# A transformer block with 32 experts on one core: output projection by feature, two gates summed on TensorE, a ninth weight place

## The chip, the cores and the metric

The kernel runs on one core of a Trainium2 chip. The metric is the device time of one execution in microseconds (us); the figure quoted is the median of three runs. TensorE is called PE below, VectorE DVE, ScalarE ACT, GpSimd POOL and SyncE SP. DVE, ACT and POOL work element by element, PE multiplies matrices, and SP issues almost all of the DMA transfers.

## The reference

One block of a model on 256 tokens of 1024 features, float32, depth 1. In outline:

```
mod = silu(c) @ w_ada + b_ada                      # 6 vectors of 1024
sh1, sc1, ga1, sh2, sc2, ga2 = split(mod)
h = rmsnorm(x, g_norm1) * (1 + sc1) + sh1
q_lat, kv_lat, k_pe, sb_qkv, gate_a, gate_b = split(h @ w_in)
o_mla = latent attention(q_lat, kv_lat, k_pe)      # 8 heads, softmax, chunk-causal
o_sb  = stick-breaking attention(sb_qkv)           # 8 heads
merged = sigmoid(gate_a) * (o_mla @ w_o_mla) + sigmoid(gate_b) * (o_sb @ w_o_sb)
x = x + ga1 * (merged @ w_out)
h2 = rmsnorm(x, g_norm2) * (1 + sc2) + sh2
x = x + ga2 * moe(h2)                              # top 4 of 32 experts
```

Each expert is a clamped SwiGLU with `w_gate_up` of 1024 x 2048 and `w_down` of 1024 x 1024, so the experts' weights are 32 x 12 MB and nearly all of what is read from memory.

## The kernel before, in words

**Weights.** Everything is streamed from memory once. First come 27 units of up to 2 MB (`load_units`, issued by SP at L174) with the modulation, projection and attention weights, through a ring of five, later six places. Then come 192 units of 2 MB for the experts (`expert_weights`, L804): per pair of experts eight units of `w_gate_up` and four of `w_down`. They go through eight places: the six of the ring and two more (`places`, L790 and L791). A unit is issued when the unit that held its place has been read for the last time.

**Order of the work.** The program is one long function. A scheduler decides the order of instructions on each engine from a simulated timeline, except where an engine is named in `ordered`; there the order of the program is kept. `ordered` holds DVE, ACT and PE in the front, DVE and PE around the last output projection, and PE in the first pair of experts. All operations of PE, DVE and ACT go through one helper and so have one line, L79; the trace tells them apart by the names of their tiles.

**Front (L178 to L452).** `x` arrives with the tokens on the partitions. 16 PE transposes (`p_xt`) turn it, and the factor of the norm is put in when the transposed tiles are copied to `xT`. The two vectors of the first norm's modulation are summed on PE (`first_sums`: eight matmuls into four 32-row strips of `p_mod`; `first_modulation`: two matmuls by ones). Float32 products are made of three matmuls in a faster type, on a high and a low half (`split`, `mm3`). `h @ w_in` for the latent and the stick-breaking columns runs in eight steps over j (`p_in`). The 32 rotary key columns are not among them; they come later as eight plain float32 matmuls (`p_kpe`, L505).

**Attention and merge (L475 to L786).** The other four modulation vectors (`ada2`: 1 and 2 for the second norm, 0 and 3 for the gates ga1 and ga2) are summed on DVE: 32 products of 128x1024 with a row sum (`modulation_sum`, L701), 16 of them for the gates, hung behind splits of weights in the gate and merge steps. The merge runs over eight feature blocks m: `merge_of` makes gate_b (`p_gb`) and both output products (`p_m`) and from them `m_hi` and `m_lo`; `project` (L759) adds the block to the output projection with the tokens on the partitions:

```
for t in range(2):
    for d in range(2):
        mm3(accs[t][d], (rows_of(m_hi, m, t), rows_of(m_lo, m, t)), w[d], m == 0, False)
```

**Router (L807 to L914).** `ga1` has been spread over all partitions (`rows_of_column`: diagonal matrices on ACT, a matmul by ones `p_row`, a copy on ACT). DVE multiplies the projection by it and adds `x`, which is loaded again (L784). 16 PE transposes (`p_ht`) make `x2T`, from which `p_lg` makes the router's logits, separately for the two halves of the tokens. `residual` puts `x` itself into the accumulators with four matmuls by the identity.

**Experts (L917 to L1142).** The tokens of four experts at a time are gathered by matmuls with one-hot matrices (`gather`, `p_xg`); each expert makes `p_gate` and `p_up` (`gate_up`), a hidden tile (`swiglu`, `hidden`) and `p_y` (`down`). `scaled` multiplies by ga2 and `combine` adds the pair's results to the tokens. In the first two pairs there are also: the broadcast of ga2 (`rows_of_column`, L1130), and the biases of the down projections (`down_biases`, L1081: one DMA of `b_down` on ACT's queue, four matmuls `acc<-rest,gwT`).

Of the kernel before, what the change touches and what calls it, by code (L numbers as in the profile page):

```python
# [36 lines left out]
UNIT = 4096  # L37

# [25 lines left out]
def block_kernel(ctx: ExitStack, tc: tile.TileContext, a, out):  # L64
# [96 lines left out]
    def load_units(n):  # L161
        ins = None
        for _ in range(n):
# [14 lines left out]
    xT = m8([128, 8, T], "xT")  # L178
    x = x8([128, 2, D], "x")
    for t in range(2):  # L180
        SP.dma_start(out=x[:, t], in_=a["x"][:, t])
# [76 lines left out]
    ss = ep.tile([128, 2], F32, name="ss")  # L258
    r1 = ep.tile([128, 2], F32, name="r1")
    scaled = s4([128, 4, 128], "scaled")  # L260
    scaled_ident, rb = scaled[:, 0:2], scaled[:, 2:4]

    def transpose(q):
        ps = [pb("p_xt") for _ in range(2)]
        for t in range(2):
            for i in range(4):
                tr(ps[t][:, i * 128:(i + 1) * 128], x[:, t, (4 * q + i) * 128:(4 * q + i + 1) * 128], ident)
        return ps

# [59 lines left out]
    h_hi, h_lo = h8(0, [128, 8, T], "h_hi"), h8(1, [128, 8, T], "h_lo")  # L329
# [9 lines left out]
    def first_modulation(j, p, acc):  # L339
# [549 lines left out]
    with tc.issue_after(counted.ins):  # L889
        for t in range(2):  # L890
            halves(t, slice(0, 256))
# [352 lines left out]
```

## Time and profile before

| | |
|---|---|
| three runs | 1193.01, 1194.36, 1196.43 us; median 1194.36 us |
| the profiled execution | 1196.56 us, of which the span of the trace is 1194.9 us |
| busy share of the span | PE 91%, DVE 33%, ACT 17%, POOL 4% |
| TensorE clock granted, mean | 0.987 of full speed |
| bytes moved | 460.96 MB, mean 386 GB/s |

The times of the rows further on are microseconds from the start of the span. A share is of the stretch named; a wait is put down to what released it last. Matmuls are pipelined: the distance from one start to the next, not the duration of one, is what it costs in a row of equal ones.

### The profile page before, as it was taken

To read this page: it belongs to the slowest core of one execution; us is meant where nothing else is said; L and a number is where in the kernel's file an instruction comes from. 1 tells how busy PE (TensorE), PEld (TensorE's weight loads), DVE (VectorE), ACT (ScalarE), POOL (GpSimd) and SP (SyncE) were. 2 spreads that over 40 slices of the span, in tenths; PEclk is the share of its full clock that TensorE was granted. 3 is DMA by queue.
4 is the path that set the end of the run, shared out by engine and by line. 5 is a ranking of instruction groups with operands and counts; after the bars stand their busy time and mean duration, and the time that the engine had idled before them with its cause. 6 is when DMAs were issued, how large, how long until landed. Compare 5 with 4: busy or idle time off the path is not lost.

```text
span 1194.9 us, 15656 instructions
## 1 busy us (share of the span) xinstructions
PE 1086.7 (91%) x6549; PEld 611.5 (51%) x6550; DVE 390.2 (33%) x863; ACT 204.7 (17%) x453; POOL 42.6 (4%) x154
## 2 busy tenths in 40 slices
PE   9989998988999999998898889888988998899877
PEld 8968777953536344453534253425352635263524
DVE  5578787762212212221222121212121212121212
ACT  3486664641000000100000000000000000000000
POOL 6000000010000000000000000000000000000000
PEclk9999998999989999999999999999999999999999
DMA  9954459889989999999999999999999999999995
GB/s 384 364 197 182 176 209 419 296 278 409 395 368 430 426 426 428 426 428 428 426 428 427 428 426 427 427 428 428 428 426 426 425 429 428 427 427 427 428 427 215
DMA packets 34267, 460.96 MB, mean 386 GB/s; under 512 B 4080, under 2 KB 4336, under 8 KB 6032
## 3 DMA queue, kind: packets, MB, share of 16 engines
q1 hardware_dynamic: 33408, 458.65, 92.1%
q10 hardware_dynamic: 784, 1.25, 0.4%
q8 instruction: 53, 0.87, 0.3%
q14 instruction: 22, 0.18, 0.0%
HBM read 458.84 MB, written 1.05 MB: 385 GB/s over the span
## 4 chain that ended last, share of the span: by engine, by line
PE 47%; DMA 47%; DVE 3%; ACT 1%; issue 1%; ACTq 0%; DVEq 0%
DMA we<-in_w_gate_up_dram 27%; DMA we<-in_w_down_dram 18%; PE p_gate L79 10%; PE p_y L79 9%; PE p_up L79 9%; PE acc L79 4%; PE p_in L79 3%; PE p_g L79 2%; PE p_gb L79 2%; PE p_xg L79 1%; PE p_m L79 1%; DMA unit<-in_stream_dram 1%; PE p_r L79 1%; PE p_z L79 1%; PE p_sc L79 1%; PE p_mod L79 1%
## 5 line engine op out<-in xcount | busy, mean ns | idle before, releaser
L79 PE MATMUL p_gate<-we,xg 128*64 128x512 f32 x1024 | 277.2, 607 | 43.1 <-DMA we<-in_w_gate_up_dram 42.5
L79 PE MATMUL p_up<-we,xg 128*64 128x512 f32 x1024 | 270.0, 593 | 0.0
L79 PE MATMUL p_y<-we,hid 128*64 128x256 f32 x2048 | 234.2, 382 | 30.7 <-DMA we<-in_w_down_dram 27.0
L79 PEld LDWEIGHTS p_y<-we,hid 128*64 128x64 f32 x2048 | 156.4, 137 | 101.1 <-DVE late L79 27.8
L79 PEld LDWEIGHTS p_gate<-we,xg 128*64 128x64 f32 x1024 | 69.5, 137 | 183.5 <-issue 103.9
L79 PEld LDWEIGHTS p_up<-we,xg 128*64 128x64 f32 x1024 | 76.8, 137 | 143.3 <-issue 143.0
L79 DVE TENSOR_SCALAR g<-p_gate 128x512 f32<-128x512 f32 x32 | 22.1, 691 | 365.2 <-PE p_gate L79 365.2
L79 DVE TENSOR_TENSOR late<-p_y,ga 64x256 f32<-64x256 f32 x128 | 54.0, 422 | 210.1 <-PE p_y L79 208.7
L79 ACT ACTIVATE s<-g 128x512 f32<-128x512 f32 x32 | 20.1, 630 | 444.3 <-DVE g L79 444.3
L79 DVE TENSOR_TENSOR lo<-unit,hi 128x512 fp32r<-128x512 f32 x114 | 74.2, 657 | 40.0 <-ACT hi L79 35.0
L79 ACT ACTIVATE hi<-unit 128x512 fp32r<-128x512 f32 x114 | 68.3, 604 | 43.6 <-PE p_gb L79 9.4
L79 PE MATMUL acc<-late,rest 128*128 128x256 f32 x256 | 62.4, 386 | 5.3 <-DVE late L79 5.3
L79 PEld LDWEIGHTS acc<-late,rest 128*128 128x128 f32 x256 | 46.1, 190 | 21.3 <-DVE late L79 9.8
L79 ACT ACTIVATE rest<-p_pw 128x512 f32<-128x512 f32 x16 | 9.6, 597 | 260.6 <-PE acc L79 148.7
L79 ACT ACTIVATE xg<-p_xg,cols 128x256 f32<-128x256 f32 x32 | 16.8, 565 | 153.8 <-PE p_xg L79 153.8
L79 DVE TENSOR_SCALAR xg<-p_xg,cols 128x256 f32<-128x256 f32 x32 | 16.7, 539 | 74.0 <-PE p_pw L79 37.3
L79 DVE SCALAR_TENSOR_TENSOR unit<-unit,cb 128x1024 f32<-128x1024 f32 x32 | 38.7, 1217 | 0.0
L79 PE MATMUL p_xg<-oh,x2h 128*128 128x256 f32 x128 | 36.1, 314 | 2.6 <-ACT xg L79 2.5
L79 PEld LDWEIGHTS p_xg<-oh,x2h 128*128 128x128 f32 x128 | 24.1, 188 | 17.5 <-issue 12.7
L79 DVE COPY hid<-p_h 128x512 f32<-128x512 f32 x32 | 22.1, 692 | 32.0 <-PE p_h L79 31.5
L79 PE MATMUL p_xg<-oh,x2l 128*128 128x256 f32 x128 | 31.9, 281 | 0.0
L79 PE MATMUL p_in<-h_hi,hi 128*128 128x256 f32 x104 | 30.6, 294 | 0.0
(332 smaller groups left out, 1138.9 us busy)
## 6 DMA issues: line engine op xcount, KB each, us to landing
we<-in_w_gate_up_dram SPq DMA_DIRECT2D x128, 2048.0 KB, 35.2
we<-in_w_down_dram SPq DMA_DIRECT2D x62, 2048.0 KB, 32.1
unit<-in_stream_dram SPq DMA_DIRECT2D x15, 2048.0 KB, 8.6
unit<-in_stream_dram SPq DMA_DIRECT2D x6, 1872.0 KB, 13.7
unit<-in_stream_dram SPq DMA_DIRECT2D x3, 1024.0 KB, 11.3
we<-in_w_down_dram SPq DMA_DIRECT2D x2, 1024.0 KB, 34.1
we<-in_w_down_dram SPq DMA_DIRECT2D x4, 512.0 KB, 25.3
unit<-in_stream_dram SPq DMA_DIRECT2D x1, 1920.0 KB, 7.9
```

The costliest lines, as they stand in the source:

```text
L79: ins = f(*args, **kw)
```

## The change

`x` is handed over with the features on the partitions and loaded straight into `xT`, both times. The first norm's sum of squares is made with matmuls by ones, and its factor for all 256 tokens is computed on 128x256 tiles. The rotary key columns join the steps of `in1`. The sums of `ada2` for the two gates go to PE (`modulation`), after m = 2 and m = 4; the DVE sums stay for the second norm's two vectors, all in the first gate's steps. The diagonals of `rows_of_column` go from ACT to POOL and the copies behind them to DVE; `ga1` is not spread any more. `project` has the features on the partitions, so that the gate ga1 is one number per partition; the sum with `xT` is `x2T` at once, and 16 matmuls by the identity turn it into the accumulators. `b_down` lies in the space of `y` now, and `pw` and `ohw` beside it. `x2h` and `xg` change places in memory, and the room of `h_hi` and `h_lo` becomes a ninth place for expert weights.

```diff
-    x = x8([128, 2, D], "x")
+    xT = x8([128, 8, T], "xT")
...
+    def first_norm():
         for t in range(2):
...
+            for k in range(4):
+                mm(acc1[3][:, 0:T], lhsT=ones, rhs=sq[:, k], start=(t + k == 0), stop=(t + k == 4))
+        v, r, u = (norms[:, i] for i in range(3))
+        V.tensor_scalar(v, acc1[3][:, 0:T], 1.0 / D, EPS, op0=OP.mult, op1=OP.add)
+        S.activation(r, v, AF.Ln)
+        S.activation(r, r, AF.Exp, scale=-0.5)
+        V.scalar_tensor_tensor(u, r, -0.5, v, op0=OP.mult, op1=OP.mult)
+        V.tensor_mul(u, u, r)
+        V.scalar_tensor_tensor(r, u, 1.5, r, op0=OP.add, op1=OP.mult)
...
             for i in range(4):
-                S.activation(diag[:, i], ident, AF.Copy, scale=col[:, 4 * d + i:4 * d + i + 1])
+                G.tensor_scalar(diag[:, i], ident, col[:, 4 * d + i:4 * d + i + 1], None, op0=OP.mult)
             p = bank("p_row")
             mm(p, lhsT=ones, rhs=diag.rearrange("p i n -> p (i n)"), start=True, stop=True)
-            S.activation(o[:, d * 512:(d + 1) * 512], p, AF.Copy)
+            V.tensor_copy(o[:, d * 512:(d + 1) * 512], p)
...
-            if j == 0 and n == 0:
-                xt1 = transpose(1)
+            if n == 3:
+                mm3(acc1[6][0:32, T:2 * T], (w[0][:, 128:160], w[1][:, 128:160]), (h_hi[:, j], h_lo[:, j]), False, j == 7)
...
+    def modulation(n):
+        accs_ = gp.tile([128, 2, 512], F32, tag="cb", name="accr", bufs=1)
+        for d in range(2):
+            w = where["ada2", (n, d)].rearrange("p (k n) -> p k n", k=8)
+            weighted_sums([w[:, k] for k in range(8)], accs_[:, d], pc("p_ada"))
+            p = pc("p_sum")
+            for i in range(4):
+                mm(p[:, i:i + 1], lhsT=accs_[:, d, i * 128:(i + 1) * 128], rhs=ones[:, 0:1], start=True, stop=True)
+            c = slice(4 * d, 4 * d + 4)
+            V.tensor_add(cols2[:, n, c], p[:, 0:4], b2[:, n, c])
...
-        for t in range(2):
-            for d in range(2):
-                mm3(accs[t][d], (rows_of(m_hi, m, t), rows_of(m_lo, m, t)), w[d], m == 0, False)
+            w.append(split(where["out", m][:, c]))
+        for f in range(8):
+            c = slice((f % 4) * 128, (f % 4 + 1) * 128)
+            mm3(acc2[f // 2][:, (f % 2) * T:(f % 2 + 1) * T], (w[f // 4][0][:, c], w[f // 4][1][:, c]),
+                (m_hi[:, m], m_lo[:, m]), m == 0 and f % 2 == 0, m == 7)
...
+        if m in (2, 4):
+            modulation(0 if m == 2 else 3)
...
-    places[5:5] = [(ring_c, 7), (ring_c, 8)]
+    places[5:5] = [(ring_c, 7), (ring_c, 8), (keep, 9)]
...
+    for f in range(8):
+        V.scalar_tensor_tensor(x2T[:, f], acc2[f // 2][:, (f % 2) * T:(f % 2 + 1) * T], cols2[:, 0, f:f + 1], xT[:, f],
+                               op0=OP.mult, op1=OP.add)
+        if f % 4 == 3:
+            accs[f // 4] = [pa(f"acc{t}{f // 4}") for t in range(2)]
+
+            for t in range(2):
+                for i in range(f - 3, f + 1):
+                    mm(accs[f // 4][t][:, (i % 4) * 128:(i % 4 + 1) * 128], lhsT=x2T[:, i, t * 128:(t + 1) * 128],
+                       rhs=ident, start=(i % 4 == 0), stop=False, skip_group_check=True)
+
+    for f in range(8):
+        g = slice(32 * (f % 4), 32 * (f % 4) + 32)
+        mm(p_lg[g, 0:T], lhsT=wr[:, f], rhs=x2T[:, f], start=(f < 4), stop=(f >= 4), skip_group_check=True)
...
-    bd = rest[0:E, 1024:2048]
+    bd = late[0:E, 0:D]
```

The change moves instructions on several engines. Three places are shown: the gates' sums, the down biases, and the loads of expert weights.

On DVE of the kernel before, in the merge, near 190 us: the gates' sums (`unit,cols<-unit,cb`) stand four in a row between splits (`lo`) and the merge's own products (`gb`, `ma`).

```order
L79 TENSOR_TENSOR lo<-unit,hi 128x512 x5
L79 SCALAR_TENSOR_TENSOR unit,cols_1240<-unit,cb 128x1024 x4
L79 TENSOR_TENSOR gb<-p_m,gb 128x256
L79 TENSOR_TENSOR ma<-p_m,gat_1238 128x256
L79 TENSOR_TENSOR lo<-unit,hi 128x512 x2
L79 SCALAR_TENSOR_TENSOR unit,cols_1240<-unit,cb 128x1024
L79 TENSOR_TENSOR lo<-unit,hi 128x512
L79 SCALAR_TENSOR_TENSOR unit,cols_1240<-unit,cb 128x1024
L79 TENSOR_TENSOR cols_1240<-cols_1240,small 128x4
L79 TENSOR_TENSOR ma<-ma,gb 128x256
```

On PE after the change, where `modulation` of the first gate has its second half: the eight matmuls of `p_ada` stand between those of `project(2)` (`acc`). DVE has no `unit,cb` row left in the merge.

```order
L80 MATMUL acc<-m_lo,hi 128x256
L80 MATMUL acc<-m_hi,lo 128x256
L80 MATMUL acc<-m_hi,hi 128x256
L80 MATMUL p_ada<-unit,scb 32x512 x8
L80 MATMUL acc<-m_lo,hi 128x256
```

So the sums leave DVE's queue and come into PE's, four groups of eight, each with four matmuls `p_sum` further on.

On PE of the kernel before, between the third expert (bias rows `bgu`) and the fourth (`p_gate`, `p_up`): the down biases.

```order
L79 MATMUL p_gate<-bgu,sel 128x512
L79 MATMUL p_up<-bgu,sel 128x512
L79 MATMUL p_pw<-ident,rest 128x128 x4
L79 MATMUL acc_1966<-rest,gwT 128x512
L79 MATMUL acc_1967<-rest,gwT 128x512
L79 MATMUL acc_1968<-rest,gwT 128x512
L79 MATMUL acc_1969<-rest,gwT 128x512
L79 MATMUL p_gate<-we,xg 64x512 x7
L79 MATMUL p_up<-we,xg 64x512 x6
```

And after the change:

```order
L80 MATMUL p_gate<-we,xg 64x512 x13
L80 MATMUL p_up<-we,xg 64x512 x12
L80 MATMUL p_gate<-we,xg 64x512
L80 MATMUL p_up<-we,xg 64x512 x2
L80 MATMUL p_gate<-we,xg 64x512 x2
L80 MATMUL p_up<-we,xg 64x512 x2
L80 MATMUL p_gate<-bgu,sel 128x512
L80 MATMUL p_up<-bgu,sel 128x512
L80 MATMUL acc_2953<-late,gwT 128x512
L80 MATMUL acc_2967<-late,gwT 128x512
L80 MATMUL acc_2954<-late,gwT 128x512
L80 MATMUL acc_2968<-late,gwT 128x512
```

The four matmuls with `gwT` are now behind the whole of the fourth expert's `p_gate` and `p_up`.

On SP of the kernel before, the first loads of expert weights, eight ahead of the first that waits for an expert (the row of four `w_down`):

```order
L784 DMA x<-in_x_dram 128x2048
L174 DMA unit<-in_stream_dram 128x4096
L804 DMA we<-in_w_gate_up_dram 128x4096
L174 DMA unit<-in_stream_dram 128x4096
L804 DMA we<-in_w_gate_up_dram 128x4096 x7
L804 DMA we<-in_w_down_dram 128x4096 x4
L804 DMA we<-in_w_gate_up_dram 128x4096 x4
```

After the change:

```order
L770 DMA xT<-in_x_dram 128x2048
L172 DMA unit<-in_stream_dram 128x4096
L790 DMA we<-in_w_gate_up_dram 128x4096
L172 DMA unit<-in_stream_dram 128x4096
L790 DMA we<-in_w_gate_up_dram 128x4096 x5
L790 DMA we<-in_w_down_dram 128x4096
L790 DMA we<-in_w_gate_up_dram 128x4096 x2
L790 DMA we<-in_w_down_dram 128x4096 x3
L790 DMA we<-in_w_gate_up_dram 128x4096 x5
```

Nine loads stand ahead of the last three of `w_down` now, with one `w_down` before the last two of `w_gate_up`.

## Rows read from the trace of the kernel before

**Rows 1.** Windows: PE, PEld, DVE, ACT, POOL busy (instructions), PEclk, DMA share, GB/s
```profile
260.00:270.00 10.00, 9.03 (x44) 3.52 (x40) 1.28 (x4) 0.84 (x2) 3.75 (x4) 1.00 0.57 211
340.00:350.00 10.00, 10.00 (x29) 2.95 (x29) 2.08 (x3) 0.00 (x0) 0.00 (x0) 0.66 0.74 318
360.00:390.00 30.00, 29.31 (x208) 18.33 (x210) 7.89 (x17) 2.40 (x5) 0.00 (x0) 1.00 1.00 428
400.00:1160.00 760.00, 686.10 (x3982) 329.32 (x3980) 161.16 (x323) 37.27 (x65) 13.78 (x51) 1.00 1.01 427
```

**Rows 2.** Timeline of SP's queue: start, us from first to last issue, loads
```profile
208.98 35.49 SPq L804 DMA_DIRECT2D we<-in_w_gate_up_dram  x7
263.41 15.05 SPq L804 DMA_DIRECT2D we<-in_w_down_dram  x4
...
349.84 29.56 SPq L804 DMA_DIRECT2D we<-in_w_gate_up_dram  x8
387.33 4.56 SPq L804 DMA_DIRECT2D we<-in_w_down_dram  x2
```

**Rows 3.** Timeline of PE in the front: start, us, matmul, count, idle before
```profile
14.86 0.28 PE L79 MATMUL p_in<-h_hi,lo 128*128 128x256 f32 x1
14.98 1.03 PE L79 MATMUL p_xt<-ident,x 128*128 128x128 f32 x8
...
18.47 0.50 PE L79 MATMUL p_mod<-ones,acc 128*128 128x1 f32 x4
...
21.13 1.07 PE L79 MATMUL p_mod<-unit,scb 128*32 128x256 f32 x16 [0.29 <-DMA unit<-in_stream_dram]
```

**Rows 4.** Timeline of PE, the rotary key columns
```profile
74.27 1.07 PE L79 MATMUL p_kpe<-hT,l 128*32 128x256 f32 x16
```

**Rows 5.** Timeline of PE in the last projection
```profile
243.14 0.40 PE L79 MATMUL acc<-lo,m_hi 128*128 128x512 f32 x1
...
245.45 0.40 PE L79 MATMUL acc<-hi,m_lo 128*128 128x512 f32 x1
```

**Rows 6.** Groups of PE's instructions, 207 to 246 us: the broadcast of ga1
```profile
L79 PE MATMUL p_row<-diag,ones 128*128 128x512 f32 x4 | 2.0, 592 | 0.0
```

**Rows 7.** Windows of the merge (columns as in group 1)
```profile
165.70:176.00 10.30, 10.10 (x80) 9.05 (x79) 7.85 (x21) 6.67 (x18) 0.00 (x0) 1.00 0.78 271
176.00:182.00 6.00, 4.08 (x19) 3.51 (x20) 4.47 (x11) 3.43 (x9) 0.00 (x0) 0.82 1.00 429
182.00:190.00 8.00, 6.18 (x33) 5.10 (x33) 2.33 (x4) 3.14 (x7) 0.00 (x0) 0.92 0.99 420
190.00:197.00 7.00, 6.53 (x31) 5.70 (x30) 5.94 (x12) 2.52 (x4) 0.00 (x0) 0.76 1.02 431
197.00:207.20 10.20, 9.25 (x60) 8.14 (x60) 9.49 (x20) 4.86 (x10) 0.00 (x0) 1.00 1.01 411
207.20:246.00 38.80, 38.74 (x259) 35.07 (x260) 30.45 (x61) 24.25 (x53) 0.00 (x0) 1.00 0.84 302
```

**Rows 8.** The page's groups: the sums on DVE (count, busy, mean ns)
```profile
L79 DVE SCALAR_TENSOR_TENSOR unit<-unit,cb 128x1024 f32<-128x1024 f32 x32 | 38.7, 1217 | 0.0
```

**Rows 9.** Timeline of PE, router and first gather
```profile
247.67 1.86 PE L79 MATMUL p_ht<-ident,x 128*128 128x128 f32 x12 [1.39 <-DVE x L79]
...
255.75 1.02 PE L79 MATMUL acc<-x,ident 128*128 128x512 f32 x2
```

**Rows 10.** Timeline of PE, the broadcast of ga2
```profile
297.39 3.78 PE L79 MATMUL p_row<-diag,ones 128*128 128x512 f32 x4 [3.61 <-ACT diag L79]
```

**Rows 11.** Timeline of POOL soon after, two copies of one shape
```profile
301.94 0.24 POOL L988 COPY rest<-rest 128x64 f32<-128x64 f32 x1 [8.28 <-PE p_pw L79]
302.39 1.09 POOL L988 COPY rest<-rest 128x64 f32<-128x64 f32 x1 [0.21 <-DVE rest L79]
```

**Rows 12.** Timeline of PE before the fourth expert
```profile
337.45 4.41 PE L79 MATMUL acc<-rest,gwT 32*128 32x512 f32 x8
341.79 5.85 PE L79 MATMUL p_gate<-we,xg 128*64 128x512 f32 x13
```

More of the change, by code (lines that the diff above doesn't have):

```diff
@@ L328, in block_kernel @@
     hT = m8([128, 8, T], "hT")
-    h_hi, h_lo = h8(0, [128, 8, T], "h_hi"), h8(1, [128, 8, T], "h_lo")
+    h = keep.tile([128, 2, 8, T], F32R, tag="w9", name="h", bufs=1)
+    h_hi, h_lo = h[:, 0], h[:, 1]
     modp = pc("p_mod")
@@ L406, in block_kernel @@
                 split_first(j + 1)
-        S.activation(wpe[:, j], where["in1", j][:, 1664:1696], AF.Copy)
         if j == 0:
@@ L501, in block_kernel @@
     p = pc("p_kpe")
-    for k in range(8):
-        g = slice(32 * (k % 4), 32 * (k % 4) + 32)
-        with tc.issue_after(last.ins):
-            mm(p[g, 0:T], lhsT=wpe[:, k], rhs=hT[:, k], start=(k < 4), stop=(k >= 4), skip_group_check=True)
-    kpeT = e384("e", 2)[:, 0:T]
-    S.activation(kpeT, p[:, 0:T], AF.Copy)
+    kpeT = e384("e", 2)[0:32, 0:T]
+    S.activation(kpeT, acc1[6][0:32, T:2 * T], AF.Copy)
     for t in range(2):
-        mm(p[:, T + t * 32:T + (t + 1) * 32], lhsT=kpeT[:, t * 128:(t + 1) * 128], rhs=fold, start=True, stop=True,
-           skip_group_check=True)
+        tr(p[:, T + t * 32:T + (t + 1) * 32], kpeT[:, t * 128:(t + 1) * 128], ident[0:32, 0:32])
     kpe = ep.tile([128, 2, 1, 32], F32, name="kpe")
@@ L762, in project @@
             c = slice(d * 512, (d + 1) * 512)
-            w.append(split(where["out", m][:, c], modulation_sum if d else None))
-        for t in range(2):
-            for d in range(2):
-                mm3(accs[t][d], (rows_of(m_hi, m, t), rows_of(m_lo, m, t)), w[d], m == 0, False)
+            w.append(split(where["out", m][:, c]))
[3 more added lines that the diff above has]
+                (m_hi[:, m], m_lo[:, m]), m == 0 and f % 2 == 0, m == 7)
     for m in range(8):
@@ L771, in block_kernel @@
             late = t8("late")
-            ga1 = late[:, 0:D]
             wr = late[:, D:D + 8 * E].rearrange("p (k e) -> p k e", k=8)
@@ L805, in expert_weights @@
         return w
+    V.tensor_mul(ws, wr, cols2[:, 2].unsqueeze(2).to_broadcast([128, 8, E]))
+    wsum = lp.tile([128, E], F32, name="wsum")
+    V.tensor_reduce(wsum, ws.rearrange("p k e -> p e k"), axis=AX.X, op=OP.add)
+    V.tensor_mul(wr, wr, cols2[:, 1].unsqueeze(2).to_broadcast([128, 8, E]))
+    p = pc("p_c0")
+    mm(p[:, 0:E], lhsT=ones, rhs=wsum, start=True, stop=True)
+    V.tensor_add(br, br, p[:, 0:E])
     weights = {0: expert_weights(0)}
@@ L878, in block_kernel, with halves @@
             counted = V.tensor_reduce(gm[:, t], hot[:, t].rearrange("p j e -> p e j"), axis=AX.X, op=OP.add)
[L880 to L887 removed]
+    def halves(t, lo, hi):
+        s, v = slice(lo, hi), accs[t][lo // 512][:, lo % 512:(hi - 1) % 512 + 1]
+        S.activation(x2h[:, t, s], v, AF.Copy, scale=rs2[:, t:t + 1])
+        V.scalar_tensor_tensor(x2l[:, t, s], v, rs2[:, t:t + 1], x2h[:, t, s], op0=OP.mult, op1=OP.subtract)
     with tc.issue_after(counted.ins):
         for t in range(2):
[L891 to L894 removed]
+            halves(t, 0, 256)
     raw = late[:, 0:D]
@@ L903, in block_kernel @@
     mm(p[:, E:2 * E], lhsT=before, rhs=gm[:, 1], start=True, stop=False)
-    ranked = mm(p[:, E:2 * E], lhsT=ones_b, rhs=gm[:, 0], start=False, stop=True)
-    with tc.issue_after(ranked.ins):
-        residual(1, 0)
+    mm(p[:, E:2 * E], lhsT=ones_b, rhs=gm[:, 0], start=False, stop=True)
     oh = one_hots()
@@ L955, in gather @@
                                              bias=cols2[:, 2, k:k + 1]))
-                if not q and not i and after:
-                    residual(1, 1)
         if after:
@@ L1172, in layout @@
     o = {}
-    o["x"] = A(i["x"][0].reshape(2, 128, D).transpose(1, 0, 2))
+    o["x"] = A(i["x"][0].T.reshape(8, 128, T).transpose(1, 0, 2))
     c = cols(i["c"][0])
```

145 lines of the change are left out of this document (44 added, 101 removed).

## The prediction

> **What bounds the kernel now.** I read the windows first. From 360 us to near the end the DMA engines are never idle: share 1.00 or more, 427 GB/s [rows 1]. A load of expert weights is 2.097 MB, so it takes 4.91 us at that rate, and the end of the kernel is the moment from which the loads follow each other without a gap, plus what is left to load, plus a tail that the change leaves alone. What PE does after that moment costs nothing while it keeps up. Before it there are holes: 211 GB/s at 260 to 270, 318 at 340 to 350 [rows 1].
>
> The timeline of SP shows which load ends the holes [rows 2]. Eight loads are issued by 244.5, one for each place. The ninth waits for the first expert on PE, until 263.41. Counting on in the order of issue, the load at 349.84 is number 24 (from 0) and the one at 387.33 number 32. If every load had its 4.91 us, the start of a gapless stream that each of them asks for would be its issue less number times 4.91: 263.41 - 39.3 = 224.1; 349.84 - 117.8 = 232.0; 387.33 - 157.1 = 230.2. The largest decides: the release at 349.84. So PE's path from the front to there counts one to one, until the load at 387.33 takes over 1.8 us lower, and that one hangs on the same path.
>
> **The change, part by part**, as a shift of that release.
>
> *Front and in1.* The first norm becomes longer (six steps on 256 columns instead of small ones), and eight transposes of 1.03 us inside the first step go. Both end at 21.13, where PE waits 0.29 for a unit anyway [rows 3], so I put the start at 0, between -0.3 and +1.0. Each of the eight steps gets three matmuls of 256 columns; one costs 0.12 by the distance of two starts (14.86 to 14.98), so 0.36 per step, and for the seven steps behind 21.13 +2.5. The separate matmuls of the rotary key, 1.07 us, go [rows 4]. Together +1.5, between +0.5 and +2.5.
>
> *Merge.* PE gets the two gates' sums: four times eight matmuls of 512 columns on a 32-column weight. The nearest row is the same with 256 columns, 1.07 us for eight; twice that, less the overlap between groups, is 2.0. The four matmuls by ones behind them are 0.8, by two of them in 0.5 at most [rows 3]. Four times 2.8 is 11.2. `project` goes from 12 matmuls of 512 columns at 0.231 (2.31 us for the ten distances from 243.14 to 245.45 [rows 5]) to 24 of 256 at 0.12, 0.05 more each, +0.4 in eight. The broadcast of ga1 goes, -2.0 [rows 6]. PE has 9.6 us more to do.
>
> What of it lies on the path? From 207.2 to 246 PE is full, 38.74 of 38.80 us; work put there costs all of itself. From 165.7 to 207.2 it isn't [rows 7]: the idle time of the five windows is 0.2 + 1.9 + 1.8 + 0.5 + 0.9 = 5.4 us, and the clock is 0.82, 0.92 and 0.76 in three of them, which costs 1.1 + 0.6 + 1.7 = 3.4. So 8.8 us could come back. DVE loses 16 sums of 1.217 us, 19.5 us, in the merge [rows 8], and it is DVE that is nearly full from 190 on (5.94 of 7.00, 9.49 of 10.20). In the printed order the second group of eight stands between matmuls of `project(2)`, so PE has it to do where it waited for splits. Against it: ACT takes its work in order, and at 182 to 190 neither DVE (2.33 of 8.00) nor ACT (3.14) was full; that hole is a matter of order and can stay. I take 7.0 of the 8.8, and the merge at +2.6, between +0.8 and +9.6.
>
> On the clock: in the three slow windows PE had been idle for 0.5 to 1.9 us, and it is at 1.00 in the two windows where it is busy for nine tenths or more [rows 7]. The Trainium skill (TensorE: Matmul & The Clock Gate, What's actually happening) says that "the default state is throttled, and activity releases the throttle". By that rule the added matmuls win all 3.4 us back and the merge ends at +0.8; the trace agrees with the rule as far as these windows go. I took half of it in the 7.0.
>
> *Router.* Of what PE does between the last projection and the first expert these go: the wait of 1.39 for DVE, 16 transposes (12 of them 1.86, so 2.5), and the pair of residual matmuls at 255.75 between two gathers, 0.8 [rows 9]; 4.7 in all. 16 float32 products by the identity come, each two passes where a transpose has one, so up to 5.0. I take 0, between -1 and +1.
>
> *Broadcast of ga2.* PE waits 3.61 us for ACT's diagonals and then needs 3.78 [rows 10]. Eight diagonals on POOL are bounded by two copies of one shape, 0.24 and 1.09 [rows 11]: 1.9 and 8.7 us where ACT's eight end inside the wait. So the price is from 0 to +5; I take +0.8, nearer the quick one, since four diagonals are enough for PE's first matmul. The slow copy is from 302.39 on, while DVE works. The Trainium skill (GPSIMD Engine Reference, Key points) speaks against this move: the engine shares its interfaces to memory with VectorE, with contention when a DVE instruction reads two inputs from there; by that rule the slow value would hold, +5, and the sum would be +2.7 instead of -1.5.
>
> *Down biases.* 4.41 us of matmuls, and behind them 13 gates in 5.85 at a clock of 0.66 [rows 1, 12], stand before the release at 349.84. They move behind the fourth expert's `p_gate` and `p_up`, so the release comes earlier by 4 us or more, of which 1.8 count until number 32 takes over. Their DMA now waits on ACT's queue for the first pair's `combine`; behind it are `p_pw` copies and `s` of the third expert, needed later. I take -1.5, between -1.8 and 0.
>
> *Ninth place.* Load number k waits for the release of k - 9 instead of k - 8, so each of the numbers above falls by one load, -4.9. The ninth load needs a hole before 263.41 and has one: eight loads end near 257, and the share is 0.57 at 260 to 270 [rows 1]. In the printed order nine loads stand ahead of the first that waits for an expert.
>
> Sum: 1.5 + 2.6 + 0 + 0.8 - 1.5 - 4.9 = -1.5 us against the profiled execution of 1196.56, so 1195.1. That execution is 2.2 us above the median of the three runs; on their scale the change gives 1194.4 - 1.5, **1193 us**. 6.4 us of gain stand against 4.9 of added work.
>
> **The rivals.**
>
> *Slower: PE's added sums find no hole.* The place is the merge before 207 us: if the splits still wait in ACT's order and PE does its new matmuls outside the waits, nothing of the 8.8 comes back, and the path gets 9.6. The sum is +5.5: 1199.9. It decides from less than 1.9 us won back. For it: 207 to 246 is full, and the hole at 182 to 190 was not DVE's. Against: the sums did stand in DVE's way.
>
> *Faster: all holes filled.* The clock stays up, the waits go, the front costs 0.5, the diagonals 0. Sum 0.5 + 0.8 + 0 - 1.8 - 4.9 = -5.4: 1189.0. For it: DVE's load in the merge falls by a third, and the clock rule above. Against: the idle time has to fall to nothing.
>
> *The ninth place holds nothing back from the stream.* If its load starts after the first expert's release, or the loads behind are late for another reason, -4.9 falls out: +3.4, 1197.8. For it: h_hi and h_lo, whose room it is, are read until the last gate_b, some 10 us before the first expert. Against: the printed order, and the hole at 257 to 263.
>
> **How the numbers follow.** A measurement of this kernel can tell 0.3% from no change, 3.6 us, so faster is below 1190.8 and slower above 1197.9. Forecast 0.42 (a fifth of it below 1190.8, little above 1197.9), all holes filled 0.26, no hole 0.22, ninth place without effect 0.10. Faster: 0.08 + 0.23 = 0.31. Slower: 0.01 + 0.20 + 0.05 = 0.26. Same: 0.43. The range goes from 1185, 4 us below the fast rival for what the down biases and the clock may give beyond, to 1201, the slow rival with a little of the price of POOL's diagonals.
>
> **What would show it.** Right: in the windows of the merge PE near full from 176 on, at a clock of 1.00, no idle above 2 us; nine loads issued before the first release of an expert; a load behind the fourth expert no longer the last one with a hole in front of it; 427 GB/s from about the same time as now. Wrong: PE's idle time at 176 to 207 unchanged beside `p_ada`; a longer wait in front of `p_row` than 3.61; a first gather more than 5 us later; or the stream of loads gapless by 345 us, which would mean that I put the merge or the front too high.

## The result, and the profile after

The changed kernel takes 1204.55 us in the median of four runs (1202.76 to 1205.36), the kernel before 1195.39 us beside it, also in four. The ratio is 1.0076, with a 95% interval of 1.0052 to 1.0099: 9.1 us slower, between 6.2 and 11.9. The profiled execution of the changed kernel took 1202.76 us, its span is 1201.1 us, 6.2 more than before. It is the quickest of its four, and the profiled execution before, 1196.56 us, lay 1.2 above the median of its kernel: so the spans differ by less than the medians.

The page of the changed kernel, the slices (about 30 us each):

```profile
PEclk9999999989898999999999999999999999999999
DMA  9945568768999999999999999999999999999995
GB/s 384 363 192 192 183 259 371 281 280 341 373 411 427 391 427 427 427 428 428 426 427 427 428 429 426 427 428 427 427 427 428 427 428 426 428 428 427 427 428 220
```

The plateau of 427 GB/s is as before [rows 1], but it begins later. The slice from 390 to 420 us still has 391 GB/s, where the kernel before was at 428 at 360 to 390 [rows 1]. The timeline of SP gives the release that ends the holes (start, microseconds from the first to the last issue, loads):

```profile
248.24 0.80 SPq L790 DMA_DIRECT2D we<-in_w_gate_up_dram  x2
273.23 11.62 SPq L790 DMA_DIRECT2D we<-in_w_down_dram  x3
287.95 37.78 SPq L790 DMA_DIRECT2D we<-in_w_gate_up_dram  x8
328.83 13.56 SPq L790 DMA_DIRECT2D we<-in_w_down_dram  x4
347.57 37.46 SPq L790 DMA_DIRECT2D we<-in_w_gate_up_dram  x8
391.62 16.23 SPq L790 DMA_DIRECT2D we<-in_w_down_dram  x4
410.96 9.32 SPq L790 DMA_DIRECT2D we<-in_w_gate_up_dram  x2
```

Nine loads are issued by 249, the tenth waits for the first expert until 273.23. Counting on from there, with the tenth as number 9, the last issue of the row at 410.96 is load 37; it starts at 419.95 (the length of a row ends with its last issue, which takes 0.33). Its number is 419.95 - 37 x 4.91 = 238.3, and it is the largest; before it was 232.0, of load 24 [rows 2]. The difference, 6.3, is the 6.2 of the spans. In the other runs below the span is this largest number plus 962.6 to 965.2 us, so it is what an edit has to move. The sum is largest in runs 4, 7 and 10, where four or more loads lie within 0.8 us of the largest number; differences under 3 us are not to be read from the number alone.

How the same places of the program moved on PE and SP, from the two traces (start of the matmul or the load named):

| place | before | after | shift |
|---|---|---|---|
| first `p_in` | 13.07 | 14.41 | +1.3 |
| last `p_in` | 63.05 | 66.03 | +3.0 |
| first `p_r` | 86.00 | 86.18 | +0.2 |
| `p_gb`, third block | 178.63 | 176.93 | -1.7 |
| last `p_m` | 239.81 | 244.84 | +5.0 |
| first gather `p_xg` | 255.10 | 261.22 | +6.1 |
| first release of a place | 263.41 | 273.23 | +9.8 |
| third expert's bias | 336.37 | 347.62 | +11.3 |
| fourth expert's bias | 358.36 | 362.65 | +4.3 |
| fifth expert's bias | 398.32 | 410.86 | +12.5 |

The front and the attention gain: the change is 1.7 ahead at the third `p_gb`. Four places lose: the merge (+6.7), the first gather up to the release (+3.7, with 1.1 more between the last `p_m` and the first gather), the broadcast of ga2 (the +9.8 becomes +11.3), and the stretch behind the fourth expert (+8.2, after a gain of 7.0).

**The merge.** Windows of the changed kernel, columns as in [rows 7]:

```profile
165.00:176.00 11.00, 11.00 (x96) 10.42 (x92) 5.56 (x11) 7.03 (x15) 0.00 (x0) 1.00 0.88 350
176.00:182.00 6.00, 5.11 (x41) 4.70 (x40) 4.21 (x10) 2.65 (x6) 0.00 (x0) 1.00 1.02 431
182.00:190.00 8.00, 5.74 (x34) 5.33 (x34) 2.59 (x4) 3.50 (x7) 0.00 (x0) 0.80 0.99 418
190.00:197.00 7.00, 7.00 (x59) 5.43 (x58) 3.32 (x7) 3.06 (x6) 0.00 (x0) 0.98 1.05 439
197.00:207.20 10.20, 10.20 (x74) 8.25 (x74) 6.80 (x10) 4.50 (x9) 3.84 (x2) 1.00 0.92 382
207.20:246.00 38.80, 38.80 (x318) 35.29 (x317) 20.97 (x42) 21.10 (x40) 0.00 (x0) 1.00 0.65 240
```

PE has 3.1 us of idle time left there instead of 5.4, and DVE is far from full (6.80 of 10.20 where it was 9.49). The hole at 182 to 190 stayed, with a clock of 0.80: there `p_m` waits 2.0 us for a split that ACT takes up only behind gate_b's exponential. The sums themselves, in the timeline of PE:

```profile
192.39 1.92 PE L80 MATMUL p_ada<-unit,scb 128*32 128x512 f32 x16
...
197.31 0.95 PE L80 MATMUL p_sum<-ones,accr 128*128 128x1 f32 x8
...
201.98 1.05 PE L80 MATMUL p_ada<-unit,scb 128*32 128x512 f32 x2
...
203.62 1.05 PE L80 MATMUL p_ada<-unit,scb 128*32 128x512 f32 x4
...
208.61 1.04 PE L80 MATMUL p_ada<-unit,scb 128*32 128x512 f32 x2
...
210.02 1.07 PE L80 MATMUL p_ada<-unit,scb 128*32 128x512 f32 x8
```

A group of eight (16 instructions) takes 1.92. The third group, which the scheduler cut into pieces of 2, 4, 2 and 8 instructions between other matmuls, takes 4.2 in all. Four groups and four times `p_sum` are 3 x 1.92 + 4.2 + 4 x 0.95 = 13.8 us by their durations, as the prediction reckons; from start to start it is 12.8.

**From the router to the first release.** Timeline of PE:

```profile
257.59 0.41 PE L80 MATMUL p_lg<-fold,late 128*128 128x32 f32 x2 [0.87 <-DVE lg L80]
259.21 0.18 PE L80 MATMUL p_pos<-gm,before 128*128 128x32 bf16 x1 [1.21 <-DVE gm L80]
260.01 0.19 PE L80 MATMUL p_pos<-gm,before 128*128 128x32 bf16 x1 [0.62 <-DVE gm L80]
...
261.22 0.55 PE L80 MATMUL p_xg<-oh,x2h 128*128 128x256 f32 x1 [0.99 <-DVE oh L80]
...
263.07 0.58 PE L80 MATMUL p_xg<-oh,x2h 128*128 128x256 f32 x1 [0.66 <-ACT xg L80]
...
266.95 1.98 PE L80 MATMUL p_gate<-we,xg 128*64 128x512 f32 x4
268.72 1.92 PE L80 MATMUL p_up<-we,xg 128*64 128x512 f32 x4
```

One short wait after the other, and from 261 on PE is nearly half as fast: `p_gate` takes 1.98, where the same four took 1.08 before. The granted clock is 0.63 at 258 to 260 and 0.50, the 1.2 GHz level, at 260 to 272. In the kernel before it was 1.00 at 260 to 270 [rows 1].

**The broadcast of ga2.** POOL's diagonals in the timeline:

```profile
305.97 5.09 POOL L316 TENSOR_SCALAR diag<-ident,cols 128x128 f32<-128x128 f32 x8 [2.48 <-DVE g L80]
```

PE of the same execution:

```profile
308.79 2.07 PE L80 MATMUL p_row<-diag,ones 128*128 128x512 f32 x2 [5.19 <-POOL diag L316]
311.12 2.08 PE L80 MATMUL p_row<-diag,ones 128*128 128x512 f32 x2 [0.25 <-POOL diag L316]
```

Eight diagonals in 5.09 us, 0.64 each in the mean; PE waits 5.19 instead of 3.61 [rows 10].

**Behind the fourth expert.** Timeline of PE:

```profile
362.65 0.50 PE L80 MATMUL p_gate<-bgu,sel 128*128 128x512 f32 x1
...
363.31 3.69 PE L80 MATMUL acc<-late,gwT 32*128 32x512 f32 x8
369.41 1.08 PE L80 MATMUL p_h<-ident,g 128*128 128x128 f32 x4 [2.40 <-DVE g L80]
371.27 5.29 PE L80 MATMUL p_y<-we,hid 128*64 128x256 f32 x32 [0.78 <-DVE hid L80]
```

Timeline of DVE, the third expert:

```profile
351.75 1.21 DVE L80 TENSOR_TENSOR late<-late,ga 32x1024 f32<-32x1024 f32 x1 [1.61 <-DMA late<-in_b_down_dram]
367.05 0.69 DVE L80 TENSOR_SCALAR u<-p_up 128x512 f32<-128x512 f32 x1 [14.08 <-PE acc L80]
```

`u` of the third expert could have started at 353 and waits 14.08 us for the matmuls of the down biases (`acc`). `gwT` sits in one of the three buffers that `g`, `s` and `u` take turns in, and keeps it until those matmuls are done, which now stand behind the fourth expert. `p_h` then waits 2.40 for `g`. Of the 8.2, 3.7 are the moved matmuls themselves, 2.4 this wait, and 2.1 are `p_h` and `p_y`, which take 1.08 and 5.29 where they took 0.60 and 3.67 before.

### The profile page after: what moved, and what is told of

It is laid out like the page before. It is cut to its first block, busy times and chain, and to the rows that moved or that the text cites. A ratio compares the mean times of both kernels' runs of the same rounds, so it can differ in the third digit from the quotient of the medians.

```text
span 1201.1 us, 15930 instructions
## 1 busy us (share of the span) xinstructions
PE 1095.9 (91%) x6719; PEld 619.8 (52%) x6720; DVE 377.6 (31%) x830; ACT 194.8 (16%) x412; POOL 53.0 (4%) x170
## 3 DMA queue, kind: packets, MB, share of 16 engines
HBM read 458.84 MB, written 1.05 MB: 383 GB/s over the span
## 4 chain that ended last, share of the span: by engine, by line
PE 59%; DMA 34%; DVE 4%; ACT 2%; issue 1%; POOL 0%; DVEq 0%; ACTq 0%; POOLq 0%
DMA we<-in_w_down_dram 34%; PE p_y L80 14%; PE p_gate L80 10%; PE p_up L80 9%; PE acc L80 7%; PE p_in L80 4%; PE p_xg L80 3%; PE p_gb L80 2%; PE p_m L80 2%; PE p_g L80 2%; PE p_z L80 1%; DVE late L80 1%; PE p_ada L80 1%; PE p_mod L80 1%; PE p_sc L80 1%
## 5 line engine op out<-in xcount | busy, mean ns | idle before, releaser
L80 PE MATMUL p_up<-we,xg 128*64 128x512 f32 x1024 | 273.2, 595 | 0.0
L80 PE MATMUL p_y<-we,hid 128*64 128x256 f32 x2048 | 236.9, 385 | 28.6 <-DMA we<-in_w_down_dram 23.6
L80 PE MATMUL acc<-late 128*128 128x256 f32 x256 | 62.4, 387 | 6.9 <-DVE late L80 6.9
L80 PEld LDWEIGHTS acc<-late 128*128 128x128 f32 x256 | 46.1, 189 | 22.6 <-DVE late L80 12.8
L80 ACT ACTIVATE late<-p_pw 128x512 f32<-128x512 f32 x16 | 9.6, 597 | 280.6 <-PE p_pw L80 229.1
L80 PE MATMUL p_in<-h,hi 128*128 128x256 f32 x224 | 42.1, 288 | 0.8 <-ACT h L80 0.7
L80 PEld LDWEIGHTS p_in<-h,hi 128*128 128x128 f32 x224 | 33.6, 183 | 4.2 <-issue 2.9
L80 PEld LDWEIGHTS p_xg<-oh,x2h 128*128 128x128 f32 x128 | 25.1, 196 | 15.9 <-issue 11.1
L80 PE MATMUL p_in<-h,lo 128*128 128x256 f32 x112 | 31.4, 281 | 0.0
```

Source lines behind the costliest of these rows:

```text
L80: ins = f(*args, **kw)
```

## The experiments

Number is the largest of issue less load times 4.91; ratios are to the kernel before, run beside each.

| run | number (load) | span | median | ratio (95%) |
|---|---|---|---|---|
| before | 232.0 (24) | 1194.9 | | 1 |
| changed | 238.3 (37) | 1201.1 | 1204.55 | 1.0076 (1.0052 to 1.0099) |
| 1: eight places | 243.9 (32) | 1207.0 | 1208.78 | 1.0109 (1.0087 to 1.0132) |
| 2: sums on DVE | 233.4 (37) | 1196.2 | 1196.50 | 1.0007 (0.9992 to 1.0022) |
| 3: fill matmuls | 237.6 (37) | 1200.2 | 1202.85 | 1.0054 (1.0033 to 1.0074) |
| 4: gwT's own buffer | 237.0 (37) | 1202.0 | 1203.67, one run | |
| 5: diagonals on ACT | 237.3 (37) | 1200.1 | 1203.32 | 1.0073 (1.0057 to 1.0088) |
| 6: 3 + 4 + 5 | 231.5 (37) | 1195.4 | 1197.71 | 1.0021 (1.0010 to 1.0032) |
| 7: 2 + 3 + 4 + 5 | 225.5 (33) | 1190.2 | 1191.96 | 0.9965 (0.9949 to 0.9981) |
| 8: before, seven places | 239.4 (23) | 1202.3 | 1203.82 | 1.0065 (1.0049 to 1.0082) |
| 9: key columns twice | 245.2 (37) | 1208.1 | 1210.29 | 1.0121 (1.0099 to 1.0143) |
| 10: 7 with eight places | 230.7 (20) | 1195.9 | 1195.97 | 0.9998 (0.9983 to 1.0013) |

**Run 1, eight places.**

```diff
-    places[5:5] = [(ring_c, 7), (ring_c, 8), (keep, 9)]
+    places[5:5] = [(ring_c, 7), (ring_c, 8)]
```

> The changed kernel with eight places instead of nine, all else kept. Theory A (the end is set by the load whose release comes latest, its issue less its number times 4.91 us; 238.4 for load 37 in the changed kernel, 232.1 for load 24 before): every load waits for one more release, so the largest of these numbers rises by up to 4.9, to about 243, and the time by 4 to 5 us, to some 1209. Theory B (the ninth place costs something itself, by the w_down load that now goes ahead of two gate_up loads): the time falls or stays, 1200 to 1205, and the first release of an expert comes earlier than 273.2.

The number rose by 5.6, the span by 5.9, the ratio by 0.0033 (about 4 us). Theory A holds: 4.9 of it are the place, and in this execution PE was also 1.2 later at the fifth expert's bias (412.05). The ninth place does what it says; the loss is elsewhere.

**Run 2, the gates' sums on DVE.**

```diff
-BY_FEATURE = (1, 2)
+BY_FEATURE = (0, 1, 2, 3)
...
-            w.append(split(where["out", m][:, c]))
+            w.append(split(where["out", m][:, c], modulation_sum if d else None))
...
-        if m in (2, 4):
-            modulation(0 if m == 2 else 3)
```

(and the same hook behind the splits of gate_b and of the output weights)

> The changed kernel with the two gates' sums on DVE again (all 32 products of 128x1024 hung behind the splits as before; no p_ada, no p_sum). Theory A (the merge is bound by PE, and the 13 us of p_ada and p_sum come back only by 4.7): the last projection ends about 6 us earlier, near 245 instead of 251.1, and the time falls by 5 to 6.5 us, to 1198 to 1199.5. Theory C (the merge is longer because of the projection by feature or the scheduler's order, not the sums): the last projection ends within 2 us of 251 and the time stays within 2 us.

The last `p_m` starts at 241.19 instead of 244.84, although this execution was 1.4 us later at the end of in1; the number fell by 4.9 and so did the span. From the third `p_gb` to the last `p_m` it is 61.3 us, as before (61.2), where the changed kernel takes 67.9. By the ratios it is 8 us, more than expected. Windows of this run, columns as in [rows 7]:

```profile
176.00:190.00 14.00, 12.35 (x89) 11.95 (x88) 8.26 (x18) 7.28 (x16) 0.00 (x0) 0.88 1.00 428
190.00:207.20 17.20, 14.72 (x119) 14.10 (x117) 16.75 (x31) 7.70 (x16) 2.06 (x2) 1.00 1.01 424
```

DVE is nearly full again at 190 to 207.2 (16.75 of 17.20) and PE waits 2.5 us there. Even so the merge ends earlier than with the sums on PE: theory A. The projection by feature stands in this run, so it isn't what made the merge longer: the 6.7 of that stretch are the sums on PE.

**Run 3, fill matmuls.**

```diff
+    def fill(p, n):
+        for _ in range(2 * n):
+            mm(p[:, 0:256], lhsT=ones, rhs=scb.rearrange("p k n -> p (k n)"), start=True, stop=True,
+               skip_group_check=True)
...
+    with tc.issue_after(routed.ins):
+        fill(p_fill, 2)
...
+    with tc.issue_after(ranked.ins):
+        fill(p_fill, 1)
...
+                if not q and not i and after:
+                    fill(p_fill, 1)
```

> The changed kernel with eight matmuls of 256 columns, whose result nobody reads, where the residual matmuls of the kernel before stood: four behind the router's last matmul, two behind the ranks, two between the first two gathers. Theory A (the residual matmuls were work in PE's waits that kept the clock up; without them PE has waits of 0.5 to 1.2 us in a row from 256 on and the clock is 0.50 at 260 to 270): the clock at 260 to 270 is 0.9 or more, the first release of an expert comes at 269 to 270 instead of 273.2, and the time falls by 2.5 to 4 us. Theory D (the clock falls for another reason, or the added work takes what it wins): the first release stays within 1 us of 273.2 and the time within 1.5 us.

Two windows of this run, and the second of them in the changed kernel (columns as in [rows 7]):

```profile
246.00:260.00 14.00, 12.52 (x107) 11.32 (x106) 8.39 (x30) 6.79 (x18) 0.00 (x0) 1.00 1.00 428
260.00:270.00 10.00, 8.41 (x45) 5.22 (x45) 8.06 (x28) 4.16 (x10) 0.49 (x2) 1.00 0.45 192
```

```profile
260.00:270.00 10.00, 7.69 (x26) 4.76 (x27) 7.29 (x24) 3.88 (x9) 0.50 (x2) 0.50 0.38 161
```

The clock is 1.00 where it was 0.50, and the first release comes at 270.93, 2.3 earlier in a run whose first gather was 1.0 later: 3.3 us won for 4 us of matmuls without a use. The release that decides, load 37, moved by 0.7 only, and the ratio by 0.0022, which the intervals don't tell from nothing. Theory A is right on the clock and the release; of the 2.3 us 1.6 were lost by load 37. Behind the broadcast of ga2 `p_pw` takes 1.06 us and the first `p_y` 4.34, against 0.69 and 3.67 in the changed kernel, and behind the fourth expert the first `p_y` takes 5.88 against 5.29: 1.6 in all. The granted clock is low in the same stretches of both executions (0.52 at 306 to 313, 0.50 at 368 to 374 us), and work that comes earlier has more of itself in them.

**Run 4, a buffer of its own for gwT.**

```diff
-        gwT = lo2([E, T], "gwT")
+        gwT = lp.tile([E, T], F32, name="gwT")
```

> The changed kernel with a buffer of its own for gwT, which shared three buffers with the activations' tiles; nothing else is changed. Theory A (u of the third expert waits 14.1 us for the buffer that gwT holds until its matmuls, which now stand behind the fourth expert; p_h then waits 2.4 us and the second expert pair's p_y runs at half clock): u is there soon after 349, no wait of p_h, the first p_y after 363 starts near 368 instead of 371.3 and takes 3.7 instead of 5.3 us; the release numbers of loads 33 and 37 fall by 3 to 5 us, and the time by 2 to 4 us, to the next largest (234.6). Theory E (the wait of p_h hangs on something else): p_h still waits over 2 us and the time stays within 1 us.

DVE of this run in the timeline, the third expert's `u`, which starts without a wait:

```profile
352.24 0.67 DVE L80 TENSOR_SCALAR u<-p_up 128x512 f32<-128x512 f32 x1
```

PE behind it:

```profile
365.73 0.60 PE L80 MATMUL p_h<-ident,g 128*128 128x128 f32 x4
366.26 3.70 PE L80 MATMUL acc<-late,gwT 32*128 32x512 f32 x8
369.88 5.36 PE L80 MATMUL p_y<-we,hid 128*64 128x256 f32 x32
```

`u` starts at 352.24 and `p_h` now runs ahead of the matmuls with gwT, without a wait. This execution was 3.0 us later at the last `p_m`, yet load 37 came 1.3 earlier: 4.3 won in between, 3.8 of it between the fourth and the fifth expert's bias. The number itself fell by 1.3 only, not by the 3 to 5 expected. But `p_y` still takes 5.36: that part of the expectation was wrong. The slow clock isn't behind the wait but behind the matmuls with gwT, which run without a gap on both sides here (windows of this run, columns as in [rows 7]):

```profile
366.00:370.00 4.00, 4.00 (x14) 1.61 (x13) 3.04 (x5) 0.63 (x1) 0.25 (x1) 1.00 1.03 438
370.00:373.00 3.00, 3.00 (x16) 1.75 (x18) 0.00 (x0) 0.00 (x0) 0.00 (x0) 0.51 0.99 421
```

The one time of this run can't tell 2 us.

**Run 5, ga2's diagonals on ACT.**

```diff
-                G.tensor_scalar(diag[:, i], ident, col[:, 4 * d + i:4 * d + i + 1], None, op0=OP.mult)
+                if on_act:
+                    S.activation(diag[:, i], ident, AF.Copy, scale=col[:, 4 * d + i:4 * d + i + 1])
+                else:
+                    G.tensor_scalar(diag[:, i], ident, col[:, 4 * d + i:4 * d + i + 1], None, op0=OP.mult)
...
-                    rows_of_column(ga2, cols2[:, 3], ps)
+                    rows_of_column(ga2, cols2[:, 3], ps, True)
```

(and the two copies behind them on ACT too, as before)

> The changed kernel with the eight diagonals of ga2 and the two copies behind them on ACT again; cb's stay on POOL and DVE. Theory A (POOL needs 5.1 us for the eight, 0.64 each, where ACT needed 2.4, and PE's wait in front of the broadcast is 5.2 instead of 3.6): PE's wait falls to 3.6 or less, everything behind it comes 1.6 to 2.0 us earlier, the largest release number falls from 238.4 to about 236.5, and the time by 1.5 to 2 us. Theory F (the wait hangs on the buffer that g holds, not on the engine): the wait stays at 5 us and the time within 1 us.

The broadcast's matmuls in this run's timeline of PE:

```profile
308.06 3.24 PE L80 MATMUL p_row<-diag,ones 128*128 128x512 f32 x4 [3.61 <-ACT diag L80]
```

The diagonals in its timeline of ACT:

```profile
306.73 2.44 ACT L80 ACTIVATE diag<-ident,cols 128x128 f32<-128x128 f32 x8 [1.54 <-DVE g L80]
```

The wait is 3.61 again, to the digit of the kernel before, and the eight diagonals take 2.44. From the second expert's bias to the last of the broadcast's matmuls it is 7.0 us instead of 9.7. The time moved by less than can be told: the last `p_m` was 2.3 later in this execution, and the ratios differ by 0.0003. Theory A holds in the trace for the wait.

**Run 6, the edits of runs 3, 4 and 5 together.**

> The changed kernel with the fill matmuls, the own buffer for gwT and ACT's diagonals for ga2 together; the gates' sums stay on PE. Theory A: the three shifts add up as far as they lie ahead of the same release (2.3 + 4 + 1.8), the largest number falls from 238.4 to 230 to 232, and the time to 1196 to 1198.5, no more than before. Theory G (the next release takes over at once): 1201 to 1203.

The number fell by 6.8 to 231.5, the time to 1197.71, 0.21% above the kernel before. The shifts add up for the most part, 6.8 of the 8.1 that theory A adds. Alone, runs 3, 4 and 5 show 0.7 to 1.3 in the number each; each of their executions was later at the last `p_m` than the changed kernel's, by 1.0, 3.0 and 2.3. The clock was not at 1.00 throughout, though the fill matmuls stand in this run as in run 3; a window of this run (columns as in [rows 7]):

```profile
259.00:262.00 3.00, 3.00 (x11) 2.24 (x10) 2.65 (x10) 1.12 (x3) 0.00 (x0) 0.50 0.98 421
```

**Run 7, the edits of run 6 and that of run 2.**

> The same three and the gates' sums on DVE again, nine places kept. Theory A: 5 to 8 us less than the run with three, the largest release number 225 to 228, and the time 1188 to 1192, below the kernel before by 4 to 8 us, of which the ninth place gives 4.9. Theory G (another bound takes over, such as the router's first gather or the tail): 1194 or more.

The number is 225.5, the median 1191.96, at the upper end of what was expected: 0.35% less than the kernel before, between 0.19 and 0.51. It is the only version that is clearly below the kernel before. Here too the clock falls once in spite of the fill matmuls, behind a wait of 1.74 us in the gathers (columns as in [rows 7]):

```profile
261.00:264.00 3.00, 3.00 (x10) 0.84 (x8) 0.10 (x1) 0.00 (x0) 0.00 (x0) 0.50 0.00 0
```

So what the fill matmuls win is not the same in every run. From the last `p_m` to the first release it is 25.1 and 25.6 us with them (runs 3 and 6) and 26.9 to 28.4 without (the changed kernel, runs 1, 4, 5 and 9), beside sums on PE; beside sums on DVE it is 27.2 with them (this run and run 10) and 27.7 without (run 2).

**Run 8, the kernel before with seven places.**

```diff
-    places[5:5] = [(ring_c, 7), (ring_c, 8)]
+    places[5:5] = [(ring_c, 7)]
```

> The kernel before with seven places for expert weights instead of eight, all else kept. Theory A (each place is worth one load, 4.91 us, in the release that decides): the largest release number rises from 232.1 to about 237, and the time by 4 to 5.5 us. Theory B (places matter only in the changed kernel, or not at all): within 1.5 us of the kernel before.

The number rose by 7.4 and the time by 0.65%, 7.8 us: more than one load. Load 23, released by the same work as load 24 before, came 2.5 us later itself, since the fourth expert's bias on PE went from 358.36 to 360.87. That was lost between the first gather, 0.5 earlier than before, and the first release, 2.6 later. Timeline of PE in this run, and a window of it (columns as in [rows 7]):

```profile
258.95 0.38 PE L79 MATMUL p_xg<-oh,x2l 128*128 128x256 f32 x1 [1.82 <-DVE x2l L79]
```

```profile
261.00:264.00 3.00, 3.00 (x8) 0.72 (x6) 1.26 (x5) 0.00 (x0) 0.45 (x2) 0.50 0.00 0
```

So the router of the kernel before, with its residual matmuls, can also fall to half the clock, with 3.2 us more between the gather and the first release. Whether the other order with seven places or the execution brought this about is open.

**Run 9, the key columns twice.**

```diff
+                mm3(acc1[6][0:32, T:2 * T], (w[0][:, 128:160], w[1][:, 128:160]), (h_hi[:, j], h_lo[:, j]), False, False)
```

> The changed kernel with the three matmuls of the rotary key columns issued twice in each of the eight steps of in1; the rotary part of the keys is counted double, so the output is not the reference's. Theory A (the path from the front to the first release has no slack: in1's end comes 3.0 us later in the changed kernel, and the stage up to p_r made it up because q's copies and the separate key matmuls left it): in1 ends 2.8 us later, near 68.9, p_r starts 2 to 3 us later than 86.2, the largest release number rises from 238.4 to 240 to 241, and the time by 2 to 3 us. Theory H (the wait for ACT in front of p_r swallows what in1 loses): p_r starts within 0.6 us of 86.2, and the time stays within 1 us.

in1 ended at 68.84, 2.8 later, and `p_r` started at 88.71, 2.5 later: the wait in front of `p_r` swallows next to nothing, and theory H falls. But the attention and the merge were laid out anew by the scheduler, the last `p_m` came 7.7 later, and the number rose by 6.9. The size of the end's shift can't be put down to the key columns.

**Run 10, run 7 with eight places** (the edit of run 1).

> The run with all four repairs (sums on DVE, fill matmuls, own buffer for gwT, ACT's diagonals for ga2), with eight places instead of nine. Theory A: the ninth place is worth one load there too, the largest release number rises from 225.6 to about 230.5, and the time by 4 to 6 us to 1196 to 1198, no better than the kernel before. Theory B (the win over the kernel before comes from the repairs, not from the place): within 2 us of 1192.

The number rose by 5.2, the time to the kernel before's (0.9998). The win of run 7 over the kernel before is the ninth place, and the four repairs do no more than make up for the rest of the change.

## Why the prediction was wrong

The way of reading held: the end is the largest release number plus 962.6 to 965.2 us, in every run. What failed were terms of the sum. Against the forecast of -1.5, 6.3 came in the number, 7.8 more: -3.2 from the front and the attention, +4.1 from the merge, +4.8 from the router, +0.7 from the broadcast of ga2 and +1.4 from the down biases with the change of the release that decides. Two of the signs that I had named for being wrong came too: a wait of 5.19 in front of `p_row`, and a first gather 6.1 later.

*Front and in1* (forecast +1.5: nothing up to 21.13, +2.5 for the steps, -1.07 for the separate key matmuls). The first two held. The first `p_in` came 1.3 later, but the `p_mod` that stood at 21.13 is at 21.60, only 0.5 later, and with seven steps of 0.36 in1 ended 3.0 later. The stage behind it became 2.8 shorter instead of 1.07: PE's wait for `vv` fell from 3.73 to 2.56, and its work by 1.6. `p_st`, from which the factor of `vv` is made, now stands ahead of most of `p_kv`, at 77.34 instead of 81.32, and q's copies left ACT for DVE; I had put in nothing for that, and no run shows which of the two did it. The granted clock behind that wait, 0.50 at 86 to 90 us before, is 1.00. By the third block of the merge the change was 1.7 ahead, 3.2 better than forecast.

*Merge* (forecast +2.6, bounds +0.8 to +9.6). It lost 6.7. Two steps are wrong. "Four times 2.8 is 11.2" measured 13.8, for the third group lost its overlap when it was cut up, and `p_sum` is 0.95. (`project` is mis-added besides: 24 matmuls at 0.12 against 12 at 0.231 are 0.9 more in eight, not 0.4.) And "I take 7.0 of the 8.8": PE's added work less the broadcast of ga1 was 12 to 13 us, so 5 to 6 came back. The rival in which no hole is filled was nearer. The argument against it that I had written down myself, ACT's order at 182 to 190, was the right one. Run 2 shows it: with the sums on DVE the merge is as long as before. My reading of the clock in [rows 7] was too smooth: at 190 to 197 PE is busy for 6.53 of 7.00 us, more than nine tenths, and the clock is 0.76. In the changed kernel it is 0.98 to 1.00 in the four windows where PE was busy throughout; the slow stretch had its cause in a wait that the added work didn't fill. The rule of the Trainium skill that I weighed there (TensorE: Matmul & The Clock Gate, What's actually happening: activity releases the throttle) agrees with these windows. It does not cover run 4, where PE is busy for all of 366 to 373 us and the clock falls to 0.51.

*Router* (forecast 0, bounds -1 to +1). It cost 4.8, and this is the worst step: "the pair of residual matmuls at 255.75 between two gathers, 0.8", counted as a gain. The first gather came 1.1 later than the projection's shift, and from there to the first release another 3.7 were lost at the clock of 1.2 GHz. The residual matmuls had stood in PE's waits; without them PE had four waits of 0.6 to 1.2 us in a row. Run 3 shows it: matmuls for nothing in the same places bring the clock back to 1.00 and the release 3.3 us forward. The size is not firm: with such matmuls the low clock lasted from nothing to some 3 us there (the kernel before, runs 3, 6, 7, 8 and 10), without them 10 to 14 us (the changed kernel, runs 1, 2, 4, 5 and 9), and run 8 lost 3.2 us all the same; so it may in part be chance that the profile before had none. I had applied the rule of the Trainium skill on activity (TensorE: Matmul & The Clock Gate, What's actually happening) to the merge alone; here it speaks against the change.

*Broadcast of ga2* (forecast +0.8, bounds 0 to +5). It cost 1.5 on the path; run 5 takes 2.7 off up to the last `p_row` and 2.1 up to the third expert's bias. The price lies between the two copies' rows, but they mixed two things. Seven of the eight diagonals take POOL 0.60 us each; the first takes 1.02, and PE waits for it:

```profile
305.97 1.02 POOL L316 TENSOR_SCALAR diag<-ident,cols 128x128 f32<-128x128 f32 x1 [2.48 <-DVE g L80]
```

DVE beside it, and, in the kernel before, DVE beside the slow copy at 302.39 [rows 11]:

```profile
305.83 0.69 DVE L80 TENSOR_TENSOR g<-g,s 128x512 f32<-128x512 f32 x1
```

```profile
302.17 1.21 DVE L79 TENSOR_TENSOR rest<-rest,ga 32x1024 f32<-32x1024 f32 x1
```

In the front, at 64 to 69 us, one diagonal of eight takes 0.99 as well, beside DVE's `lo<-unit,hi` at 67.04. Each time DVE works on two tiles. The rule of the Trainium skill on the shared interfaces (GPSIMD Engine Reference, Key points: contention with DVE instructions that have two inputs in SBUF) agrees with these rows. But it gives 0.4 of the 5.09 us; the rest is POOL's own 0.60 for a diagonal, where ACT does all eight in 2.44.

*Down biases* (forecast -1.5). The move gave 7.0 up to the fourth expert's release, more than the 4 written down, and took 8.2 right behind it. The sentence "behind it are `p_pw` copies and `s` of the third expert, needed later" looked at ACT's queue; the wait was in a buffer, gwT's, that DVE's `u` takes its turn in (run 4). And 1.8 us "until number 32 takes over" was read as a floor of the gain, not as the place where the loss would count: with load 24 out of the way the releases behind the fifth expert decide, and PE was 12.5 late there.

*Ninth place* (forecast -4.9). Runs 1 and 10 give 5.6 and 5.2: this term held.

Together, at the fifth expert: PE 12.5 later, less 4.9, is 7.6 on the number of what was load 32 and is load 33, 230.2 before [rows 2] and 237.8 after. The number that decided before stood 1.8 higher, and the one that decides now is 0.5 above 237.8, so 6.3 are left: the difference of the spans. The medians add 3 us, because the profiled execution before was slow for its kernel and the one after quick. No rival reached this: the slower one had 1199.9, and the time lies above the range.

## What to carry to other kernels

Matmuls that look like mere work on the path may be what fills PE's waits and keeps its clock at 2.4 GHz; before taking them out, look what PE does between the waits that are left, and read more than one execution, for the clock does not fall alike in all. A step that is moved behind other work keeps its buffers for as long: list who takes turns in them. Where prefetched loads set the end, write each release as issue less number times the load's time; it says which part of the program an edit must move, and how far until the next one takes over.

## What the runs showed of the hardware that was not expected

- PE's clock was 0.50 at 260 to 272 us with no wait longer than 1.21 us: ahead of it stood waits of 0.50, 0.87 and 1.21, and PE was busy for 0.81 of the 2 us from 256 on. With eight products of 256 columns, 4 us, in such waits it stayed at 1.00 in run 3 and fell for some 3 us in runs 6, 7 and 10.
- Behind the eight matmuls with gwT, on 32 rows of the array, the next `p_y` took 5.36 instead of 3.7 us although PE had no idle time before, during or after them (run 4: clock 0.51 at 370 to 373). In the kernel before 13 gates ran at half clock behind them too [rows 12].
- Eight matmuls on 32-column weights (16 instructions) cost 1.92 us in one piece and 4.2 in pieces of 2, 4, 2 and 8 instructions, some 1.05 for each piece whatever its size.
- A 128x128 product by a column took POOL 0.60 us, and 0.99 to 1.02 where DVE worked on two tiles beside it; ACT took 0.31 in a row of eight, and POOL itself 0.30 for a plain copy with conversion of that size.
